# A state-space mixer whose TensorE order is written out by hand: eight products per run, dense slices between them, and a projection that ends half by half

## The chip, the core and the metric

The kernel runs on one core of a Trainium2 chip. It works with five engines, each with a queue of its own that it takes in order: TensorE (matmuls, PE in the profile, with its weight loads as PEld), VectorE (DVE), ScalarE (ACT), GpSimd (POOL) and SyncE (SP), which here issues nearly all transfers between device memory and the on-chip memory. The metric is the device time of one execution in microseconds; a kernel is told by the median of its runs.

## What is computed

One layer of a streaming encoder on a sequence of 1024 positions of width 1024, in float32. One input projection feeds two branches, whose outputs are gated, added and projected; a SwiGLU sub-layer follows.

```python
proj = h @ w_in
y_a = sparse_mla_attention(...) @ w_o_attn
y_b = ssd_mixer(z, xbc, dt_raw, ...) @ w_o_ssd
mix = (sigmoid(g_a) * y_a + sigmoid(g_b) * y_b) @ w_out
x = x + gate_m * rmsnorm(mix, post_norm_mix)
f = (silu(u_gate) * u_up) @ w_ffn_out
x = x + gate_f * rmsnorm(f, post_norm_ffn)
```

The change lies in the stretch that computes the state-space branch: for 8 groups of 4 heads the sequence is worked through in chunks. Within a chunk, with decay matrix `Lmat` and inputs `X`, and with the state `prev` that earlier chunks leave:

```python
CB = einsum('bclgn,bcsgn->bcgls', Cc, Bc)
y_diag = einsum('bcgls,bcgrls,bcsgrp->bclgrp', CB, Lmat, X)
states = einsum('bclgn,bcgrl,bclgrp->bcgrpn', Bc, decay, X)
y_off = einsum('bclgn,bcgrpn,bcgrl->bclgrp', Cc, prev, exp(a_cum))
y = y_diag + y_off + d_skip * xh
return rmsnorm(y * silu(z), ssd_norm)
```

The kernel uses chunks of 256 positions instead of 64, which gives the same sums.

## The kernel before

Activations lie with channels on the 128 partitions and positions along the free dimension, in two halves of 512 positions (`b` is 0 or 1). A dense product is made in float32 accuracy from three matmuls per 128 x 128 tile: each operand is split into a high part (a copy in the format fp32r) and a low part (the rest), and high x high, high x low and low x high are added. A half of one output tile over 1024 inputs is thus 24 matmuls of 128 x 128 by 128 x 512 (`dense`, or `dense_steps`, a generator that yields after every six). Splits are made by `split_to` (high on ScalarE at L246, low on VectorE or GpSimd at L247); weights come through `Stream` (transfer at L150, high on ScalarE at L151, low on GpSimd at L152), up to three split tiles at a time.

On-chip memory is handed out from arenas, each a number of equal slots: H with 32 slots of 512 columns, Q with 26 of the same size, R with 8 of 1024, EV with 9 of 512. A slot is used again when all readers of the tile in it are through.

After the attention come 32 steps, one for each pair of group and chunk, group outermost. A step has two parts, both generators:

- `ssd_in` loads B, C and x (`ld`, L961 and L962) and the cumulated decay, spread over all partitions (`al`, L967), takes relu and exp of the decay on ScalarE (L972, L973, L975), and makes on TensorE the product of B and C (`pcb`, L978 and L979), the transposed x (`px`, L989) and, but for the last chunk, the transposed B (`pbn`, L998). VectorE masks pcb (`cbm`, L981), multiplies it into the decay, which gives M in the tiles `al` and `M` (L983), and scales x (`X`, L991); GpSimd weighs X with the decay to the end of the chunk (`Xd`, L1002). It yields after each piece: four pieces.
- `ssd_out` loads z and the decay from the start of the chunk into one tile (`zy`, L1013 and L1016), multiplies M and X (`pyd`, L1022 and L1023, products of half the array's columns, four with 256 columns and four with 128), Xd and B (`pst`, L1029), and the state and C (`pyo`, L1034). VectorE adds these up (L1036, L1037, L1041), GpSimd multiplies by z (L1043), the result is stored (`d_y`, L1044), its squares are summed for the norm (L1047, L1053), and the state is brought forward (L1057, L1059). It has four pieces as well; the first ends in the middle of pyd.

`weave` calls the pieces of `ssd_in` for one step and of `ssd_out` for the step before in turn, and calls the generator `beside` between them, four times per step. `beside` is dense work that the mixer doesn't need: eight tiles of the input projection for one of the gates (`pw`, two halves each, input Hs, the split h, which fills all 32 slots of H), then the loads and splits of the attention's output (`atl`, L1078, into H), then eight tiles of the attention's output projection (`poa`, two halves each, evacuated at L1087). That is 32 products of four slices each, 128 slices.

This order of calls isn't the order on the engines. A planner, which simulates the program with costs of its own, takes the traced instructions and orders each engine's queue anew, as operands, slots and engines come free in its simulation. The context `in_order` chains the instructions of an engine in the order in which they were traced, and so takes this freedom away on that engine for the code inside; instructions from outside can still be put between. The mixer stands in an `if True:` without it.

After the mixer `y_load` loads y, half by half, scales and splits it (`yh` on ScalarE at L1125, `yw` on VectorE at L1126, into H, 32 slots for the 16 tiles of a half), and `merge` multiplies it by `w_o_ssd` (`pos`, 48 matmuls per tile, weights through the same `Stream`).

Of the kernel before, what the change touches and what calls it, by code (L numbers as in the profile page):

```python
# [11 lines left out]
F32R = mybir.dt.float32r  # L12
# [13 lines left out]
D_INNER, SSD_HEADS, GROUPS = 2048, 32, 8  # L26
# [12 lines left out]
NCH = L // QC  # L39
LAST = ((0, 0, 512), (1, 0, 256), (1, 256, 256))  # L40
FFN_GROUPS = [4, 4, 4, 4, 3, 3]
EARLY = 18

COLS = {}
_n = 0
# [22 lines left out]
def build(tc, a, dbg=None, stop=99, slots=None):  # L68
# [9 lines left out]
    H_ = Arena(ctx, tc, "H", n_slots["H"], 512)  # L78
# [7 lines left out]
    def bank_d(name):  # L86
        return pd.tile([P, 512], F32, name=name, tag="d", bufs=3)
# [7 lines left out]
    def half(b):  # L95
        return slice(512 * b, 512 * b + 512)
# [74 lines left out]
    def col_tile(w):  # L171

        kt = w.shape[1]
        return [(w[:, k:k + min(4, kt - k)], min(4, kt - k)) for k in range(0, kt, 4)]
# [55 lines left out]
    def dense_steps(o, b, w, xs, n=6):  # L230

        i = 0
        for (hi, lo), k0, ks in w:
            for j, k in enumerate(ks):
                for wt, xi in ((hi, 0), (hi, 1), (lo, 0)):
                    T.matmul(o, wt[:, k0 + j, :], xs[k][xi][b], start=i == 0, stop=i == 23)
                    i += 1
                    if i % n == 0 and i < 24:
                        yield

    def wpieces(ks, n=4):

        return [(W.next(), 0, ks[i:i + n]) for i in range(0, len(ks), n)]
# [5 lines left out]
    def split(alloc, src, name, shape=None, lo_eng=None):  # L249
        hi = alloc(name + "h", shape, F32R)  # L250
        lo = alloc(name + "l", shape, F32R)
        split_to(src, hi, lo, lo_eng)
        return hi, lo
# [569 lines left out]
    def weave(x, nx, y, ny, z=iter(()), nz=0, lead=1):  # L823

        i = j = k = 0
        while i < nx or j < ny:
            if j >= ny or (i < nx and i * ny <= j * nx * lead):
                next(x, None)
                i += 1
            else:  # L830
                next(y, None)
                j += 1
            while k < nz and k * (nx + ny) < nz * (i + j):
                next(z, None)
                k += 1
        for g in (x, y):
            for _ in g:
                pass
# [167 lines left out]
    def ssd_out(c, g, z):  # L1006
# [12 lines left out]
        for j in range(2):  # L1019
            for e in range(2):  # L1020
                o = pyd[64 * e:64 * e + 64, 256 * j:256 * j + 256]
                T.matmul(o, X[:, 0, 2 * j + e], M[j][:, e], start=True, stop=False, skip_group_check=True)  # L1022
                T.matmul(o[:, 128:256], X[:, 1, 2 * j + e], M[2][:, 2 * j + e], start=False, stop=True, skip_group_check=True)  # L1023
            if j == 0:
                yield
        if c < NCH - 1:
            pst = bank("pst")
            for t in range(2):
# [33 lines left out]
    def beside():  # L1062

        for t in range(8):
            W.plan(col_tile(a["w_in"][57 + t]))
            w = wpieces(ks8)
            for b in BS:
                p = bank_d("pw")
                yield from dense_steps(p, b, w, Hs)
                o = EV("g")  # L1070
                S.activation(o, p, AF.Copy)
                SP.dma_start(d_gb[t][:, half(b)], o)
                yield
        AT = [([None, None], [None, None]) for _ in range(KT)]
        for b in BS:
            for k in range(KT):
                t = EV("atl")
                SP.dma_start(t, d_att[k][:, half(b)])  # L1078
                AT[k][0][b], AT[k][1][b] = split(H_, t, "at", lo_eng=G if k % 2 else V)
        for t in range(8):  # L1080
            W.plan(col_tile(a["w_o_attn"][t]))
            w = wpieces(ks8)
            for b in BS:
                ya = EV("ya")
                p = bank_d("poa")
                yield from dense_steps(p, b, w, AT)
                V.tensor_copy(ya, p)  # L1087
                SP.dma_start(d_ya[t][:, half(b)], ya)
                yield

    filler = beside() if stop != 3 else iter(())
    if True:
        prev = None
        for s_ in [(c, g) for g in range(GROUPS) for c in range(NCH)] + [None]:
            z = {}
            weave(ssd_in(*s_, z) if s_ else iter(()), 4 if s_ else 0, ssd_out(*prev) if prev else iter(()), 4 if prev else 0, filler, 4)
            prev = s_ and (*s_, z)
        for _ in filler:
            pass
# [20 lines left out]
    def y_load(b, ks, places):  # L1120
        for k in ks:
            t = EV("yl")
            SP.dma_start(t, d_y[k][:, half(b)])
            yh, yw = places("yh", dt=F32R), places("yw", dt=F32R)
            S.activation(yh, t, AF.Copy, scale=col("ssd_norm", k))  # L1125
            V.scalar_tensor_tensor(yw, t, col("ssd_norm", k), f(yh), op0=OP.mult, op1=OP.subtract)  # L1126
            YB[b][k] = ([yh] * 2, [yw] * 2)
# [121 lines left out]
        t = R(name, (P, 2, 512), F32R)  # L1249
        return t[:, 0], t[:, 1]  # L1250

    y_load(0, range(16), H_)
    rys = []
    for b in BS:
        rys.append(wp.tile([P, 4, P], F32, name="rys", tag=("uraw", "uh")[b], bufs=1).rearrange("p k m -> p (k m)"))
        S.activation(rys[b], rbank(ysq[b], D_INNER), AF.Copy)
    MG = merge(0, in_r)
    y_load(1, range(16), H_)
    x1 = []
    for _ in residual_steps(0, *mixed(0, MG), x1):  # L1260
        pass
# [259 lines left out]
```

## Time and profile before

| | us |
|---|---|
| runs, median (lowest to highest) | 2464.05 (2463.94 to 2467.35) |
| span of the profiled execution | 2459.8 |
| median of the runs above that span | 4.25 |
| TensorE busy in the span | 2383.1 (97%) |
| VectorE, ScalarE, GpSimd busy | 1496.3, 1183.7, 1022.3 |
| first pcb of the mixer to its last | 1141.7 to 1486.1 |
| first and last poa | 1301.6 and 1458.1 |
| first pos | 1463.2 |

In the views of the profile L12 is line 12 of the kernel; a row names the tile that is written and those that are read. Matmuls overlap in the pipeline, so the distance from start to start tells what one costs, not its duration; a product in plain float32 shows as two records. In views by stretch of time a row has the busy time of each engine, the granted clock of TensorE (1.00 is full speed), the busy share of the 16 DMA engines and GB/s. A row of waits has the waiting instruction, what released it, the sum, how many, and the longest. Rows of transfers have the size in KB and the median time from issue to landing.

### The profile page before, as it was taken

What the parts mean: (1) busy time and instruction counts of PE and PEld (TensorE: products, weight loads), DVE (VectorE), ACT (ScalarE), POOL (GpSimd) and SP (SyncE); (2) the same over time, 40 slices, a digit from 0 to 9 for tenths busy, and PEclk for the clock granted to TensorE, in tenths of its full rate; (3) what the DMA queues carried; (4) which work ended last, traced back from release to release, by engine and by line L of the source; (5) the groups of instructions that cost most, each with busy time, mean ns of one, the idle gap of its engine ahead of it and who ended that gap; (6) DMA issues with size and microseconds to landing.
All of it is one profiled execution on the core that took longest, in us unless ns stands there. A gap on an engine that the chain in (4) does not pass through costs nothing. (4 is left out here: it accounts for less than half of the span.)

```text
span 2459.8 us, 34881 instructions
## 1 busy us (share of the span) xinstructions
PE 2383.1 (97%) x11946; PEld 1931.1 (79%) x11946; DVE 1496.3 (61%) x3050; ACT 1183.7 (48%) x2285; POOL 1022.3 (42%) x829
## 2 busy tenths in 40 slices
PE   7999999999999999999999999999999999999996
PEld 5788888888788887777776767888777888888886
DVE  4566775698745556765558666455476666552336
ACT  4446665567445545556566565544454222352211
POOL 2722112222234334553336335656676555432233
PEclk9999999999999999999999999999999999999998
DMA  7224122523212222223768775654465444253132
GB/s 268 99 77 130 65 73 78 155 87 103 86 67 92 102 99 91 93 84 123 223 215 260 228 246 172 231 186 161 168 208 171 160 145 163 99 190 113 48 99 90
DMA packets 212834, 341.25 MB, mean 139 GB/s; under 512 B 21249, under 2 KB 85425, under 8 KB 212657
## 3 DMA queue, kind: packets, MB, share of 16 engines
q1 hardware_dynamic: 211936, 338.45, 41.6%
q8 instruction: 94, 1.54, 0.3%
q14 instruction: 84, 0.68, 0.1%
q10 hardware_dynamic: 720, 0.58, 0.1%
HBM read 254.77 MB, written 87.32 MB: 139 GB/s over the span
## 5 line engine op out<-in xcount | busy, mean ns | idle before, releaser
L152 POOL TENSOR_TENSOR wlo<-wraw,whi 128x512 fp32r<-128x512 f32 (+1 forms) x282 | 380.7, 1351 | 769.4 <-ACT whi L151 698.5
L151 ACT ACTIVATE whi<-wraw 128x512 fp32r<-128x512 f32 (+1 forms) x282 | 175.4, 623 | 319.0 <-PE pfo L226 110.5
L1283 PE MATMUL p<-xh,wr 128*128 128x512 f32 x880 | 274.4, 391 | 3.8 <-DVE g L1333 3.6
L1283 PEld LDWEIGHTS p<-xh,wr 128*128 128x128 f32 x880 | 165.8, 188 | 39.1 <-DVE g L1333 4.0
L1277 POOL TENSOR_TENSOR wr<-a,wr 128x512 fp32r<-128x512 f32 x110 | 152.7, 1402 | 103.6 <-ACT wr L1276 70.6
L1283 PE MATMUL p<-xl,wr 128*128 128x512 f32 x440 | 171.8, 391 | 0.0
L778 ACT ACTIVATE lg<-lg,mx 128x256 f32<-128x256 f32 (+7 forms) x128 | 98.2, 769 | 74.7 <-DVE mx L775 73.5
L1276 ACT ACTIVATE wr<-a 128x512 fp32r<-128x512 f32 x110 | 67.7, 628 | 123.1 <-PE p L1283 98.0
L226 PE MATMUL pfo<-ah,wlo 128*128 128x512 f32 x304 | 118.1, 389 | 0.0
L226 PE MATMUL pfo<-al,whi 128*128 128x512 f32 x304 | 117.9, 389 | 0.0
L226 PE MATMUL pfo<-ah,whi 128*128 128x512 f32 x304 | 117.8, 389 | 0.0
L317 POOL TENSOR_TENSOR adaw<-adaw,cs 128x512 f32<-128x512 f32 x64 | 66.7, 1044 | 114.7 <-DMA adaw<-ada_w 109.4
L1398 DVE TENSOR_TENSOR facc<-facc,pfo 128x512 f32<-128x512 f32 x64 | 43.9, 686 | 112.0 <-PE pfo L226 112.0
L1283 PE MATMUL p<-h2h,wr 128*128 128x512 f32 x352 | 111.1, 393 | 0.0
L638 ACT ACTIVATE junk<-acc,cand__2203 128x1024 bf16<-128x1024 f32 (+2 forms) x96 | 86.2, 898 | 45.5 <-DVE cand__2203 L681 28.0
L226 PE MATMUL pos<-yw,whi 128*128 128x512 f32 x256 | 101.7, 397 | 3.6 <-DVE yw L1126 3.6
L226 PE MATMUL pos<-yh,whi 128*128 128x512 f32 x256 | 101.4, 396 | 1.7 <-ACT yh L1125 1.7
L226 PE MATMUL pos<-yh,wlo 128*128 128x512 f32 x256 | 101.5, 397 | 1.1 <-POOL wlo L152 1.1
L589 DVE SCALAR_TENSOR_TENSOR acc<-rel,widx,acc 128x384 f32<-128x384 f32 (+2 forms) x90 | 87.0, 986 | 24.9 <-ACT rel L584 24.7
L584 ACT ACTIVATE rel<-prel 128x512 f32<-128x512 f32 (+3 forms) x160 | 77.3, 524 | 48.4 <-PE prel L583 44.8
L1283 PEld LDWEIGHTS p<-xl,wr 128*128 128x128 f32 x440 | 83.0, 189 | 17.4
L799 PE MATMUL pt<-ident,lg 128*128 128x128 f32 x576 | 87.4, 277 | 7.1 <-ACT lg L778 6.6
(573 smaller groups left out, 6978.2 us busy)
## 6 DMA issues: line engine op xcount, KB each, us to landing
wraw<-w_in SPq DMA_DIRECT2D x130, 256.0 KB, 2.6
a<-w_ffn_in SPq DMA_DIRECT2D x124, 256.0 KB, 3.0
adaw<-ada_w SPq DMA_DIRECT2D x64, 256.0 KB, 2.7
al<-d_ac SPq DMA_DIRECT2D x32, 512.0 KB, 5.8
wraw<-w_o_ssd SPq DMA_DIRECT2D x64, 256.0 KB, 3.2
al<-d_a SPq DMA_DIRECT2D x44, 256.0 KB, 5.3
d_a<-g SPq DMA_DIRECT2D x40, 256.0 KB, 2.5
ada<-ada_p SPq DMA_DIRECT2D x16, 512.0 KB, 6.5
```

Of the source, the lines that this page charges most:

```text
L151: behind(S.activation(hi[:, :kt], raw[:, :kt], AF.Copy))
L152: behind(G.tensor_tensor(lo[:, :kt], raw[:, :kt], f(hi[:, :kt]), op=OP.subtract))
L226: T.matmul(o, wt[:, k0 + i, :], xs[k][xi][b][:, sl], start=pi == 0 and i == 0 and wt is hi and xi == 0, stop=pi == len(pcs) - 1 and i == l ...
L317: behind(G.tensor_tensor(t, t, cs[:, 4 * h:4 * h + 4, None].to_broadcast([P, 4, P]), op=OP.mult))
L584: S.activation(rel[:, 512 * b:512 * b + w_], pr[:, 0:w_], AF.Relu)
L589: V.scalar_tensor_tensor(acc[i][:, 0:n], rel[:, 0:n], ws, acc[i][:, 0:n], op0=OP.mult, op1=OP.add)
L638: S.activation(jk, y, AF.Sign, scale=-1.0, bias=a_, accum_out=o)
L778: S.activation(lg[:, 0:n], lg[:, 0:n], AF.Exp, scale=-1.0, bias=m, accum_out=mx[:, 3:4])
L799: T.transpose(ptv[:, hh, t, :], PR[hh, t][:, j * P:(j + 1) * P], ident)
L1276: S.activation(w[:, 0], src, AF.Copy)
L1277: G.tensor_tensor(w[:, 1], src, f(w[:, 0]), op=OP.subtract)
L1283: T.matmul(p, w[:, wi, i], X[x][i][xi], start=start and i == 0 and k == 0, stop=i == 3 and k == 2, skip_group_check=True)
```

## The change

Three things are done together. The mixer's TensorE instructions are put into `in_order`, so they go in the traced order. For that order the yield inside pyd is taken out, so all eight products of a step follow each other, `ssd_out` counts as three pieces, and the dense work is called four and three times in turn instead of four. Whatever of it is left after the last step follows there, inside the same order. The attention's projection takes tiles 0 to 4 with both halves each, and then tiles 5 to 7 with the first half and once more with the second, for which their weights are loaded again. The split input of the projection goes to Q for the first four tiles of the first half, and the split y of tiles 8 to 11 of the first half goes to Q as well.

```diff
+POA_BOTH = 5
+AT_IN_Q = 4
+Y_IN_Q = range(8, 12)
...
                 T.matmul(o[:, 128:256], X[:, 1, 2 * j + e], M[2][:, 2 * j + e], start=False, stop=True, skip_group_check=True)
-            if j == 0:
-                yield
...
-                AT[k][0][b], AT[k][1][b] = split(H_, t, "at", lo_eng=G if k % 2 else V)
-        for t in range(8):
-            W.plan(col_tile(a["w_o_attn"][t]))
-            w = wpieces(ks8)
-            for b in BS:
-                ya = EV("ya")
...
+                AT[k][0][b], AT[k][1][b] = split(Q if b == 0 and k < AT_IN_Q else H_, t, "at", lo_eng=G if k % 2 else V)
+        for ts, bs in [((t,), BS) for t in range(POA_BOTH)] + [(range(POA_BOTH, 8), (b,)) for b in BS]:
+            for t in ts:
+                W.plan(col_tile(a["w_o_attn"][t]))
+                w = wpieces(ks8)
+                for b in bs:
+                    ya = EV("ya")
...
-    if True:
+    with in_order(mybir.EngineType.PE):
         prev = None
-        for s_ in [(c, g) for g in range(GROUPS) for c in range(NCH)] + [None]:
+        for n, s_ in enumerate([(c, g) for g in range(GROUPS) for c in range(NCH)] + [None]):
             z = {}
-            weave(ssd_in(*s_, z) if s_ else iter(()), 4 if s_ else 0, ssd_out(*prev) if prev else iter(()), 4 if prev else 0, filler, 4)
+            weave(ssd_in(*s_, z) if s_ else iter(()), 4 if s_ else 0, ssd_out(*prev) if prev else iter(()), 3 if prev else 0,
+                  filler, 4 - n % 2)
...
-            yh, yw = places("yh", dt=F32R), places("yw", dt=F32R)
+            where = places(k)
+            yh, yw = where("yh", dt=F32R), where("yw", dt=F32R)
...
-    y_load(0, range(16), H_)
+    y_load(0, range(16), lambda k: Q if k in Y_IN_Q else H_)
...
-    y_load(1, range(16), H_)
+    y_load(1, range(16), lambda k: H_)
```

More of the change, by code (lines that the diff above doesn't have):

```diff
@@ L1078, in beside @@
                 SP.dma_start(t, d_att[k][:, half(b)])
-                AT[k][0][b], AT[k][1][b] = split(H_, t, "at", lo_eng=G if k % 2 else V)
-        for t in range(8):
-            W.plan(col_tile(a["w_o_attn"][t]))
-            w = wpieces(ks8)
-            for b in BS:
-                ya = EV("ya")
[L1085 to L1089, printed above, removed]
+                AT[k][0][b], AT[k][1][b] = split(Q if b == 0 and k < AT_IN_Q else H_, t, "at", lo_eng=G if k % 2 else V)
[5 more added lines that the diff above has]
+                    ya = EV("ya")
+                    p = bank_d("poa")
+                    yield from dense_steps(p, b, w, AT)
+                    V.tensor_copy(ya, p)
+                    SP.dma_start(d_ya[t][:, half(b)], ya)
+                    yield
     filler = beside() if stop != 3 else iter(())
-    if True:
+    with in_order(mybir.EngineType.PE):
         prev = None
-        for s_ in [(c, g) for g in range(GROUPS) for c in range(NCH)] + [None]:
+        for n, s_ in enumerate([(c, g) for g in range(GROUPS) for c in range(NCH)] + [None]):
             z = {}
-            weave(ssd_in(*s_, z) if s_ else iter(()), 4 if s_ else 0, ssd_out(*prev) if prev else iter(()), 4 if prev else 0, filler, 4)
+            weave(ssd_in(*s_, z) if s_ else iter(()), 4 if s_ else 0, ssd_out(*prev) if prev else iter(()), 3 if prev else 0,
+                  filler, 4 - n % 2)
             prev = s_ and (*s_, z)
```

## The prediction

> **What bounds the kernel now.** I read the page first, then the busy time by stretch around the state-space mixer, then the waits of TensorE in the two stretches that stood out, then the order of time on TensorE within one step.
>
> ```profile
> span 2459.8 us, 34881 instructions
> ```
>
> ```profile
> core 0: us, PE busy (x) PEld busy (x) DVE busy (x) ACT busy (x) POOL busy (x), PEclk, DMA share, GB/s
> 1290.00:1320.00 30.00, 24.81 (x118) 17.58 (x117) 24.02 (x29) 20.14 (x42) 19.37 (x14) 0.89 0.98 310
> 1460.00:1480.00 20.00, 14.71 (x65) 9.14 (x64) 15.40 (x23) 17.03 (x35) 4.75 (x4) 0.74 1.00 325
> 1180.00:1290.00 110.00, 110.00 (x598) 85.81 (x598) 63.64 (x101) 67.21 (x149) 40.93 (x34) 1.00 0.68 218
> 1340.00:1450.00 110.00, 110.00 (x599) 85.88 (x598) 74.17 (x117) 59.12 (x132) 43.90 (x36) 1.00 0.72 230
> ```
>
> In the two long stretches TensorE has no idle time at all and the full clock: there only fewer or cheaper TensorE instructions can gain, and no other engine is near its limit. The two short stretches are seams. At 1290 to 1320 it idles 30.00 - 24.81 = 5.2 us, and the granted clock of 0.89 costs about 0.11 x 24.81 = 2.7 us more: 7.9 us. At 1460 to 1480 it idles 5.3 us and loses 0.26 x 14.71 = 3.8 us to the clock: 9.1 us. Both have the DMA engines at a share of 0.98 and 1.00. The waits name the seams:
>
> ```profile
> PE poa L236 <- ACT ath L246: 3.2, 2, 3.0
> PE poa L236 <- POOL atl L247: 1.2, 1, 1.2
> ```
>
> ```profile
> PE pos L226 <- DVE yw L1126: 3.6, 3, 2.3
> PE pos L226 <- ACT yh L1125: 1.7, 1, 1.7
> ```
>
> The first is the attention's projection waiting for its split input, which can be written only once the split h (Hs) has left arena H. The second is the merge's first product waiting for the split of y, which takes H after the projection is through with it.
>
> At 1460 the Trainium skill ("TensorE: Matmul & The Clock Gate", Why this matters for your kernels) would say otherwise: it lets the clock fall after idle gaps of more than about 3 us between bursts. The longest wait here is 2.3 us, and the clock fell to 0.74 all the same, so the row decides; by the rule the second seam would be worth only its 5.3 us of idle time, and the sum below would be 12.2 us in place of 16 (2451.8). Since the row contradicts it, that case gets no chance of its own.
>
> **The order within a step.** These are consecutive rows of TensorE in one step, dense slices at both ends.
>
> ```profile
> 1186.88 0.39 PE L236 MATMUL pw<-h5h,wlo 128*128 128x512 f32 x1
> 1187.11 0.39 PE L236 MATMUL pw<-h6h,whi 128*128 128x512 f32 x1
> 1187.42 0.66 PE L1022 MATMUL pyd<-al,X 128*64 128x256 f32 x4
> 1187.91 0.40 PE L1023 MATMUL pyd<-M,X 128*64 128x128 f32 x4
> 1188.23 0.70 PE L978 MATMUL pcb<-ld 128*128 128x256 f32 x2
> 1188.77 0.38 PE L979 MATMUL pcb<-ld 128*128 128x128 f32 x2
> 1189.08 0.66 PE L1022 MATMUL pyd<-al,X 128*64 128x256 f32 x4
> 1189.56 0.40 PE L1023 MATMUL pyd<-M,X 128*64 128x128 f32 x4
> 1189.89 0.66 PE L989 MATMUL px<-ident,ld 128*128 128x128 f32 x4
> 1190.38 1.03 PE L1034 MATMUL pyo<-ld,state 128*128 128x256 f32 x4
> 1191.25 0.38 PE L998 MATMUL pbn<-ident,ld 128*128 128x128 f32 x2
> 1191.38 0.48 PE L236 MATMUL pw<-h6l,whi 128*128 128x512 f32 x1
> 1191.70 0.40 PE L236 MATMUL pw<-h6h,wlo 128*128 128x512 f32 x1
> ```
>
> The planner cuts the half-width products (128*64) into two runs with other work between. A dense matmul takes 0.23 us from start to start; 256 columns of a full-width product take 0.87 / 4 = 0.22 us (pyo), 128 columns 0.49 / 4 = 0.12 (px). Into a half-width run it takes 0.31 instead of 0.23, so 0.08 more; inside, the L1022 part takes 0.49 where two steps of 0.22 are due, 0.05 more; out of it 0.32 where two of 0.12 are due, 0.08 more. A run of its own thus costs about 0.2 us. Going from full-width state-space work to dense costs nothing that shows: from 1191.25 to 1191.70 are 0.45 us, which two steps of 0.11 and one of 0.23 fill.
>
> **The change, part by part.** *Eight products per run* removes one run in each of 32 steps: 32 x 0.2 = 6.4 us (4.8 to 7.7 for 0.15 to 0.24 each), on the path because TensorE has no idle time there. *Fixed order, slices between* adds no instruction. It puts the slices of six, four and three in turn, between the pieces, so the dense work no longer runs ahead: 116 of its 128 slices are used up by the 33 turns, and 12, three products of 24 matmuls or 3 x 24 x 0.23 = 16.5 us, come after the last state-space product. They are not extra work; they lie where the second seam is. *Half by half* for t = 5, 6, 7 lets the first half's split input go before these three products start; its slots in H, the eight slots of H that the projection no longer uses now that four k lie in Q, and Q for k = 8 to 11 then take the split y of twelve k ahead of time.
>
> ```profile
> L1125 ACT ACTIVATE yh<-yl,vec x32: 705/722/752, 1462.4 to 1602.4; 128x512 fp32r<-128x512 f32 x32
> L1126 DVE SCALAR_TENSOR_TENSOR yw<-yl,vec,yh x32: 735/748/1871, 1463.1 to 1605.8; 128x512 fp32r<-128x512 f32 x32
> ```
>
> Four of the twelve can go earlier still. The eight k that wait for the first half take 8 x 0.75 = 6 us on VectorE and less on ScalarE, inside the 16.5 us; the last four take 3 us while the merge's first product works on the twelve before them (36 x 0.23 = 8.3 us). So the second seam goes whole: 9.1 us, at least 5 if loads of y come late, since the DMA engines are full there.
>
> The three tiles of weights are loaded twice: six more loads of 256 KB with these splits,
>
> ```profile
> L152 POOL TENSOR_TENSOR wlo<-wraw,whi 128x512 fp32r<-128x512 f32 (+1 forms) x282 | 380.7, 1351 | 769.4 <-ACT whi L151 698.5
> L151 ACT ACTIVATE whi<-wraw 128x512 fp32r<-128x512 f32 (+1 forms) x282 | 175.4, 623 | 319.0 <-PE pfo L226 110.5
> ```
>
> 6 x 1.35 = 8.1 us on GpSimd and 6 x 0.62 = 3.7 on ScalarE. Both have a third or more of the time free in the long stretches, and behind a lo part at 1.35 us stand 12 matmuls, 2.8 us: nothing on the path. Were that cover gone, the six lo parts would cost up to 8 us.
>
> *Split input in both arenas.* Four of the first half's eight k can be split into Q before Hs is gone, and since the slices now come one product per step, the other slots of Hs come free a step before they are needed. What stays is the 16 x 0.26 = 4.2 MB of loads. The mixer's own traffic rises as its steps get shorter:
>
> ```profile
> L989 PE MATMUL px<-ident,ld x128: 272/273/328, 1144.3 to 1488.7; 128*128 128x128 f32 x128
> ```
>
> That is 31 steps in 344.4 us, 11.1 us each. A new step is 3.5 slices of 6 x 0.23 = 4.8 us and state-space products of about 4.1 (from 1187.42 to 1191.47 above, less 0.2, with pst in three of four steps): 8.9 us. The DMA share of 0.70 becomes 0.70 x 11.1 / 8.9 = 0.87, and near the seam four steps ask for 4 x 8.9 us x 280 GB/s + 4.2 MB, about 14 MB, or 43 us at the 325 GB/s of the fullest stretch, against 36 us; what is loaded ahead covers a part. I take 4.5 of the 7.9 us as won (0 to 7.9).
>
> **What the fixed order can cost.** The planner no longer fills a late operand with dense work. Two chains have to fit a step of 8.9 us. The first goes from pcb through VectorE and ScalarE to the next pyd:
>
> ```profile
> 1243.74 0.38 PE L979 MATMUL pcb<-ld 128*128 128x128 f32 x2
> ...
> 1253.65 0.66 PE L1022 MATMUL pyd<-al,X 128*64 128x256 f32 x4
> ...
> 1257.52 1.03 PE L1034 MATMUL pyo<-ld,state 128*128 128x256 f32 x4
> ```
>
> ```profile
> 1244.16 0.56 DVE L981 TENSOR_TENSOR cbm<-pcb,mask 128x384 f32<-128x384 f32 x1 [0.83 <-PE pcb L979]
> ...
> 1248.66 1.21 DVE L983 TENSOR_TENSOR al<-al,cbm 128x1024 f32<-128x1024 f32 x1
> ```
>
> ```profile
> 1246.08 1.04 ACT L975 ACTIVATE al<-al 128x1024 f32<-128x1024 f32 x1
> ```
>
> M is done 5.8 us after pcb (1249.87 - 1244.12) and pyd follows 3.8 us later. In the new order pyo, px, pbn and three slices lie between: 0.9 + 0.5 + 0.2 + 4.1 = 5.7 us. That just holds; 3 of the 5.8 us are the exponent, which can go earlier, so the chain could be 2.6 us. The second chain is the reload of zy:
>
> ```profile
> 1241.78 0.37 SPq L1044 DMA_DIRECT2D d_y<-zy  x1
> 1247.32 0.37 SPq L1013 DMA_DIRECT2D zy<-d_z  x1
> 1247.74 1.24 SPq L1016 DMA_DIRECT2D zy<-d_ea  x2
> ```
>
> ```profile
> d_y<-zy SPq DMA_DIRECT2D x32, 256.0 KB, 5.3
> zy<-d_ea SPq DMA_DIRECT2D x48, 128.0 KB, 3.3
> ```
>
> The next z is issued the moment that the store has landed, with everything behind it on SP's queue held for these 5 us, so slots are what limits the loads. The second ea lands at about 1252 and is used after pyo, at 1258.5: some 6 us of slack over two steps. Two steps shrink by 4.4 us, which leaves 1.5 to 2, less whatever fuller DMA engines add. So both chains fit with little room. I charge 4 us of new waits, 0.12 us a step; the ends are 0 and 22 (below).
>
> **The sum** against the profiled span: -9.1 (second seam) - 4.5 (first) - 6.4 (runs) + 4 (new waits) = -16.0 us, 2443.8. The runs' median stands 2464.05 - 2459.8 = 4.25 us above the span, so **2448 us**.
>
> **Rivals.** *Half of it*: the first seam stays, since the DMA engines are full, and of the second 5 us go: -5 - 6.4 + 4 = -7.4, 2456.7. For it: shares of 0.98 and 1.00 in both seams. Against it: part of the loads now comes ahead.
>
> *The reload of zy sets the step.* If landings lengthen by 1.5 us each at a share of 0.87 (5.3 to 6.8, 3.3 to 4.8), the loop of two steps is 22.2 - 6 + 3.0 = 19.2 us, 9.6 a step: 0.7 x 32 = 22 us given back, -20 + 22 = +2, 2466. For it: SP stands still 5 us a step as it is. Against it: 218 GB/s and 230 GB/s gave the same TensorE, with no wait.
>
> *Slower*: pyd waits for M in every step, because the planner leaves the exponent after pcb as now. From a chain of 5.7 + 20 / 32 = 6.3 us upward it eats all the gain of 20 us; at 6.7 us it costs 32 x 1.0 = 32, +12, 2476. For it: 5.8 us today, and ScalarE is the engine that also evacuates the dense products. Against it: SP issues the loads as soon as slots come free (its rows above), so al is there ahead of pcb and the exponent can move forward.
>
> **Numbers.** Forecast 0.42, more than that (no new waits, both seams whole, -23) 0.05, half of it 0.18, zy's loop 0.16, slower 0.19. A measurement of this kernel tells about 0.2%, 5 us, from no change. Faster: the first two and nine tenths of the third, 0.63; same: zy's loop and the rest of the third, 0.18; slower 0.19. The range goes from 2438 (all won and a little from the planner's new order elsewhere) to 2471, which leaves out the worse two thirds of the slower case; the forecast's own is 2441 to 2455.
>
> **What would show it.** In the changed profile: L1022 in runs of eight records with no pcb between; no wait of pos for yh or yw over 1 us, and the last poa after the last pyo; the granted clock at 1.00 where the merge starts; the first wait of poa on ath shorter than 3.0 us; px from first to last over some 280 to 290 us instead of 344. Waits of pyd on L983, of pcb on ld, or idle TensorE of more than 5 us inside the mixer would be the new waits. The forecast is wrong if the mixer's steps stay above 9.9 us, for then nothing is won.

## The result, and the profile after

The changed kernel takes **2493.2 us** (median of 4 runs, 2492.2 to 2494.3) against 2463.99 us before: a ratio of 1.0118, 95% interval 1.0103 to 1.0132. The forecast was 2448, with a range up to 2471. The page of the changed kernel begins with its span; before it was 2459.8 us.

```profile
span 2492.5 us, 34910 instructions
```

Busy time of the changed kernel in four stretches from the mixer to the merge (columns as in the prediction: busy time and instructions of each engine, granted clock, share of the DMA engines, GB/s):

```profile
1180.00:1290.00 110.00, 100.39 (x569) 80.10 (x569) 75.17 (x106) 69.94 (x158) 46.03 (x34) 0.98 0.69 218
1290.00:1320.00 30.00, 26.22 (x153) 20.91 (x153) 22.38 (x32) 16.10 (x37) 11.59 (x9) 1.00 0.68 197
1320.00:1450.00 130.00, 109.42 (x580) 85.75 (x580) 87.69 (x125) 72.48 (x159) 58.12 (x43) 0.93 0.71 227
...
1480.00:1520.00 40.00, 35.95 (x171) 29.55 (x172) 15.91 (x28) 14.24 (x27) 17.47 (x15) 0.93 0.43 140
```

Before, TensorE was busy all through 1180 to 1290 and 1340 to 1450 and idle only in the two seams. Now every stretch shown has idle time. The share of the DMA engines hardly moved (0.69 and 0.71 in the first and third row, against 0.68 and 0.72 in the long stretches before). The same view over the whole of the mixer and both seams, first before and then after:

```profile
1130.00:1530.00 400.00, 387.44 (x2077) 295.57 (x2076) 261.99 (x401) 238.45 (x513) 167.00 (x131) 0.98 0.69 218
```

```profile
1130.00:1530.00 400.00, 355.69 (x1949) 280.30 (x1948) 256.92 (x394) 229.36 (x499) 163.42 (x123) 0.97 0.67 212
```

Idle time grew by 387.4 - 355.7 = 31.7 us, nearly the whole loss of 32.7 us in the spans. The clock adds about 0.03 x 355.7 - 0.02 x 387.4 = 3 us, rounded as these clocks are. Over the whole span TensorE is busy for 2382.9 us against 2383.1 before, so its idle time (2492.5 - 2382.9 against 2459.8 - 2383.1) grew by 32.9 us: the loss is idle time. The steps of the mixer, which were to shrink to 8.9 us, take (1486.4 - 1150.6) / 31 = 10.8 us:

```profile
L992 PE MATMUL px<-ident,ld x128: 270/272/273, 1150.6 to 1486.4; 128*128 128x128 f32 x128
```

The waits of TensorE between 1130 and 1560 in the changed kernel say where (time, how often, longest):

```profile
PE pst L1030 <- POOL Xd L1005: 21.8, 11, 5.0
PE pyd L1025 <- DVE al L986: 10.2, 7, 2.2
PE poa L239 <- ACT ath L249: 4.5, 1, 4.5
PE pyd L1025 <- DVE X L994: 2.7, 3, 1.7
PE pos L229 <- ACT yh L1129: 2.4, 1, 2.4
PE pos L229 <- DVE yw L1130: 0.7, 1, 0.7
```

The largest, pst (the state's product) waiting for Xd, was in no term of the forecast. The waits of pyd for M (al), which it did reckon with, come second. The waits of both seams (poa, pos) are still there.

What stands behind it, in one step of the changed kernel (start, duration, engine, line; rows of four engines, in order of time, others left out at the dots):

```profile
1209.99 0.60 PE L992 MATMUL px<-ident,ld 128*128 128x128 f32 x4
...
1211.70 0.68 DVE L994 TENSOR_TENSOR X<-px,dt 128x512 f32<-128x512 f32 x1
...
1213.01 0.88 DVE L1042 SCALAR_TENSOR_TENSOR zy<-ld,dsk,zy 128x256 f32<-128x256 f32 x2
...
1214.02 1.27 POOL L1044 TENSOR_TENSOR zy<-zy 128x512 f32<-128x512 f32 x1 [2.00 <-DVE zy L1042]
...
1214.65 0.44 PE L1026 MATMUL pyd<-M,X 128*64 128x128 f32 x4
1215.25 1.04 POOL L1005 TENSOR_TENSOR Xd<-X,decay 128x512 f32<-128x512 f32 x1
1215.32 0.63 ACT L1048 ACTIVATE ysqt<-zy 128x512 f32<-128x512 f32 x1 [4.25 <-POOL zy L1044]
1215.86 0.36 ACT L1003 ACTIVATE bn<-pbn 128x256 f32<-128x256 f32 x1
...
1216.37 1.11 PE L1030 MATMUL pst<-Xd,bn 128*128 128x256 f32 x4 [1.28 <-POOL Xd L1005]
```

X is ready at 1212.38, but on GpSimd Xd stands behind the product of y with z of the step before (L1044), for which the engine stood idle 2.00 us until VectorE had done zy at L1042. Xd ends at 1216.29 and pst starts at once. On ScalarE the other operand, bn, stands behind ysqt, which waits for the same product. The Trainium skill ("Perfetto Trace Analysis", Tensor Engine Instruction) calls the execution queues of ScalarE, VectorE and GpSimd strict FIFO; this row agrees, for X was ready 2.9 us before Xd started.

The trace shows the same in all eleven waits of pst for Xd: between X and Xd GpSimd runs the product with z. In three of them nothing else stands there. In seven a low weight part (wlo, L155, about 1.3 to 2.3 us) comes in as well, and in the longest, of 5.0 us, two splits of the attention's output (atl). So it is the whole queue ahead of Xd that makes it late, with the product with z in every case.

Before, the corresponding rows were these (kernel before, same view):

```profile
1233.88 0.65 PE L989 MATMUL px<-ident,ld 128*128 128x128 f32 x4
...
1235.34 1.42 POOL L1002 TENSOR_TENSOR Xd<-X,decay 128x512 f32<-128x512 f32 x1 [1.57 <-DVE X L991]
...
1240.46 1.29 POOL L1043 TENSOR_TENSOR zy<-zy 128x512 f32<-128x512 f32 x1
...
1244.86 1.13 PE L1029 MATMUL pst<-Xd,bn 128*128 128x256 f32 x4
```

There Xd stood ahead of the product with z, and pst came 11.0 us after px, 8 us after Xd was done. The change took out the yield between the two runs of pyd. That joined the runs, but it also pulled pst, which is written behind them, from the second piece of a step into the first: it is now asked for before the next step's px, and in the median it starts 6.4 us after its own px instead of 10.3 (table below).

### The profile page after: what moved, and what is told of

It reads as the page before. It is cut to its first block, busy times and chain, and to the rows that moved or that the text cites. A ratio compares the mean times of both kernels' runs of the same rounds, so it can differ in the third digit from the quotient of the medians.

```text
span 2492.5 us, 34910 instructions
## 1 busy us (share of the span) xinstructions
PE 2382.9 (96%) x11946; PEld 1942.2 (78%) x11946; DVE 1500.9 (60%) x3050; ACT 1188.7 (48%) x2291; POOL 1036.9 (42%) x835
## 5 line engine op out<-in xcount | busy, mean ns | idle before, releaser
L155 POOL TENSOR_TENSOR wlo<-wraw,whi 128x512 fp32r<-128x512 f32 (+1 forms) x288 | 390.7, 1357 | 739.7 <-ACT whi L154 675.4
```

The costliest lines, as they stand in the source:

```text
L155: behind(G.tensor_tensor(lo[:, :kt], raw[:, :kt], f(hi[:, :kt]), op=OP.subtract))
```

## The experiments

All times are medians of four to twelve runs, with the ratio to the kernel before on the same chip and its 95% interval. The px row of each kernel (first to last of the transposes, 31 steps) gives the length of a step.

**First batch: which part of the change costs the time.** a_order_only keeps the fixed order, the runs of eight and the turns, and drops the halves and the arenas. b_halves_only does the opposite. c_run8_only is the kernel before with the yield taken out. d_pst_late is the changed kernel with pst put behind px, in the third piece.

```diff
--- changed kernel
+++ a_order_only
-POA_BOTH = 5
-AT_IN_Q = 4
-Y_IN_Q = range(8, 12)
+POA_BOTH = 8
+AT_IN_Q = 0
+Y_IN_Q = range(0)
```

> The fixed TensorE order, the runs of eight and the slices four and three in turn, but the projection with both halves of each tile together, its weights loaded once, and every split input in H, as before the change. Queue theory (the fixed order meets the order that the planner gave GpSimd, VectorE and ScalarE: Xd stands behind the product with z on GpSimd, M behind other work, and TensorE has nothing else to do): the waits of pst and pyd inside the mixer stay, some 40 us of them, the second seam is open again, 2490 to 2503 us. Load theory (fuller DMA engines and the reload of zy make operands late): the same total, but with waits that trace back to transfers. Halves theory (the second loading of weights, SP's queue and the arenas cost the time): 2455 to 2466 us.

```diff
--- changed kernel
+++ b_halves_only
+            if j == 0:
+                yield
...
-    with in_order(mybir.EngineType.PE):
+    if True:
...
-            weave(ssd_in(*s_, z) if s_ else iter(()), 4 if s_ else 0, ssd_out(*prev) if prev else iter(()), 3 if prev else 0,
-                  filler, 4 - n % 2)
+            weave(ssd_in(*s_, z) if s_ else iter(()), 4 if s_ else 0, ssd_out(*prev) if prev else iter(()), 4 if prev else 0,
+                  filler, 4)
```

> The projection half by half with its weights loaded twice for three tiles, and the split inputs in both arenas, but no fixed order, the yield inside pyd and four slices a step as before the change. Queue and load theories: no waits of pst or pyd on TensorE, 2458 to 2470 us, as the planner again fills with dense work; the seams may move by a few us either way. Halves theory: most of the 29 us, 2480 us or more.

```diff
--- kernel before
+++ c_run8_only
-            if j == 0:
-                yield
...
-            weave(ssd_in(*s_, z) if s_ else iter(()), 4 if s_ else 0, ssd_out(*prev) if prev else iter(()), 4 if prev else 0, filler, 4)
+            weave(ssd_in(*s_, z) if s_ else iter(()), 4 if s_ else 0, ssd_out(*prev) if prev else iter(()), 3 if prev else 0, filler, 4)
```

> Only the yield inside pyd is taken out (and three pieces counted); the planner orders TensorE freely, everything else as before the change. If a half-width run of its own costs 0.2 us, 32 fewer give -6.4 us, 2458 us, all theories alike; 2462 or more would say that the runs are not worth what the records of one step gave, or that the planner cuts them again.

```diff
--- changed kernel, ssd_out
+++ d_pst_late
-        if c < NCH - 1:
-            pst = bank("pst")
-            for t in range(2):
-                T.matmul(pst[:, 0:256], z["bn"][:, t], z["Xd"][:, t].rearrange("p h n -> p (h n)"), start=t == 0, stop=t == 1)
         yield
...
         yield
+        if c < NCH - 1:
+            pst = bank("pst")
+            for t in range(2):
+                T.matmul(pst[:, 0:256], z["bn"][:, t], z["Xd"][:, t].rearrange("p h n -> p (h n)"), start=t == 0, stop=t == 1)
         sq = Q("ysqt", (P, 2, 256))
```

> The changed kernel with pst moved in the fixed order from right behind pyd to behind px, some 4 us later in the step. Queue theory: the 22 us of waits of pst for Xd go, and no more than a third of them come back as waits of pyd or pyo; 2468 to 2478 us. Load theory: Xd isn't what is late, so other waits take their place, 2488 us or more.

Measured: a 2496.4 us, 1.0122 [1.0101, 1.0143]; b 2480.7, 1.0061 [1.0040, 1.0081]; c 2505.7, 1.0162 [1.0143, 1.0181]; d 2475.9, 1.0045 [1.0029, 1.0062].

So a has the whole loss, with the same waits (pst for Xd 16.9 us, pyd for M 10.3): the halves and arenas are not needed for it and do not mend it. By themselves (b) they lose 15 us, which lies at the edge of what the halves theory said (2480 or more), so they are not free where the planner orders TensorE. No wait of pst is among b's; its waits lie elsewhere: pyd for M 6.9 us, poa for ath 6.0, pos 5.4 for a weight's high part and 4.3 for y. Why they come was not tried. And d wins back 17 of the 29 us. Its largest waits of TensorE in the same stretch:

```profile
PE pyd L1025 <- DVE al L986: 15.4, 13, 2.2
PE poa L239 <- ACT ath L249: 7.2, 1, 7.2
PE pyd L1025 <- DVE X L994: 3.2, 1, 3.2
```

No wait of pst is left, and that for M has grown from 10.2 to 15.4 us: the second chain comes forward where the first is mended. c was the worst miss, since it was to win the 6 us of the runs. Its rows of the attention's projection and of px, then the last stretch of its mixer:

```profile
L236 PE MATMUL poa<-ath,whi x128: 387/389/502, 1291.6 to 1427.6; 128*128 128x512 f32 x128
```

```profile
L989 PE MATMUL px<-ident,ld x128: 272/273/273, 1152.1 to 1545.1; 128*128 128x128 f32 x128
```

```profile
1500.00:1560.00 60.00, 34.69 (x192) 26.33 (x190) 36.49 (x59) 29.41 (x62) 19.27 (x17) 0.84 0.46 149
```

With seven pieces in a turn and no order held, the planner used the dense work up by 1428, and the mixer ran on until 1545, at the end nearly without cover: 25 of 60 us idle and a clock of 0.84. Waits of pst for Xd are there as well (5.9 us, none before), although no order is held. What the missing piece does to the planner was not tried further.

**Second batch: the late operand, and the loads.** f puts Xd on VectorE. g joins the first two pieces of ssd_in, so that pcb comes ahead of the pyd of the step before. h adds to g loads that are written earlier (four attention inputs two tiles, that is four products, ahead; twelve loads of y ahead of the last three products). In the cut of h, `at_load` is the loop of these loads made a function, and `y_load` is moved up unchanged. i is the changed kernel without the loads of ea: it leaves out the factor that they bring.

```diff
--- changed kernel
+++ f_xd_on_dve
-            G.tensor_tensor(Xd, X, decay[:, 2 * c:2 * c + 2, hs, None].to_broadcast([P, 2, 4, 64]), op=OP.mult)
+            V.tensor_tensor(Xd, X, decay[:, 2 * c:2 * c + 2, hs, None].to_broadcast([P, 2, 4, 64]), op=OP.mult)
```

> The changed kernel with Xd made by VectorE (about 0.7 us) instead of GpSimd; TensorE's order is untouched. Queue theory: Xd no longer stands behind the product with z and the low weight parts, so the 22 us of waits of pst go; VectorE gets 0.7 us a step more, so the waits of pyd may grow by some us: 2470 to 2482 us. Load theory: X or other operands are late, and the waits stay: 2488 us or more.

```diff
--- changed kernel, ssd_in and the loop
+++ g_pcb_first
             S.activation(m, m, AF.Exp, scale=-1.0)
-        yield
         pcb = bank("pcb")
...
-            weave(ssd_in(*s_, z) if s_ else iter(()), 4 if s_ else 0, ssd_out(*prev) if prev else iter(()), 3 if prev else 0,
+            weave(ssd_in(*s_, z) if s_ else iter(()), 3 if s_ else 0, ssd_out(*prev) if prev else iter(()), 3 if prev else 0,
```

> The changed kernel with the first two pieces of ssd_in made one, so that in the fixed order pcb of a step goes ahead of pyd of the step before, and px and pbn move up with it: the way from pcb to the next pyd and from px to the next pst gets some 3 us longer, while the work stays the same. Queue theory: both kinds of waits inside the mixer go, what stays are the seams: 2448 to 2462 us. Load theory: pcb needs its loads 3 us earlier, so waits of pcb for ld appear, 2485 us or more.

```diff
--- g_pcb_first
+++ h_early_loads
         for t in range(8):
+            if t == 6:
+                at_load(0, range(AT_IN_Q))
             W.plan(col_tile(a["w_in"][57 + t]))
...
+        y_load(0, range(12), lambda k: Q if k in Y_IN_Q else H_)
         for _ in filler:
             pass
...
-    y_load(0, range(16), lambda k: Q if k in Y_IN_Q else H_)
+    y_load(0, range(12, 16), lambda k: H_)
```

> As the kernel with pcb first, and the loads at both seams are traced earlier: the first four tiles of the attention's output two tiles of the gate projection ahead, and twelve tiles of y ahead of the three last products. If the seams stay open because the planner puts these loads behind others on SP's queue, the waits of poa on ath and of pos on yh shrink by 5 to 12 us against the kernel with pcb first: 2438 to 2452 us. If the DMA engines are what is full there, nothing changes by more than 3 us.

```diff
--- changed kernel, ssd_out
+++ i_no_ea
-        if c:
-            for e in range(2):
-                SP.dma_start(yt[64 * e:64 * e + 64],
-                             d_ea[c, hs].rearrange("(j e) l -> e j l", e=2)[e:e + 1].to_broadcast([64, 2, QC]))
...
-            V.tensor_tensor(ytf, ytf, pyo, op=OP.mult)
+            V.tensor_tensor(ytf, zc.rearrange("p j l -> p (j l)"), pyo, op=OP.mult)
```

> The changed kernel without the 48 loads of the decay from the start of the chunk: the product of state and C is multiplied by z's tile instead, which leaves that part of the computation out. The reload of zy then has one load of 3.3 us less and the DMA engines 14% less of the mixer's traffic. Load theory: most of the 29 us come back, 2465 to 2475 us. Queue theory: the waits of pst and pyd stay as they are, 2486 to 2495 us.

Measured: f 2495.6 us, 1.0119 [1.0090, 1.0148]; g 2467.6, 1.0015 [1.0003, 1.0026]; h 2466.3, 1.0010 [1.0001, 1.0020]; i 2492.7, 1.0121 [1.0100, 1.0142].

i speaks against the loads: with 48 loads of 128 KB gone the share of the DMA engines between 1180 and 1450 falls from 0.70 to 0.63, but TensorE's idle time there is the same (34.0 and 34.5 us) and the waits stay (pst for Xd 16.8 us, pyd for M 10.3). f missed, and its waits say why:

```profile
PE pst L1030 <- ACT bn L1003: 13.5, 8, 3.2
PE pyd L1025 <- DVE al L986: 12.3, 7, 2.5
```

The wait went over to bn, pst's other operand, which stands directly behind ysqt on ScalarE in all eight, as in the rows of the changed kernel. g has no wait of pst, 11.6 us for M and steps of (1458.7 - 1150.9) / 31 = 9.9 us; it came out 6 us above its expectation. h closed the second seam, but its 1.3 us less than g are within the intervals: new waits came near the first seam, pbn for cbm 4.1 us, pyd for M up to 5.2 us.

**Third batch: the order by itself, M, and the mends together.** j is the kernel before with TensorE's order fixed as it is written, nothing else. m is the changed kernel with the runs of eight undone. k is g with VectorE's order fixed too. l takes g, pst of d and the loads of y of h together.

```diff
--- kernel before
+++ j_fixed_only
-    if True:
+    with in_order(mybir.EngineType.PE):
--- changed kernel
+++ m_runs_of_four
+            if j == 0:
+                yield
...
-            weave(ssd_in(*s_, z) if s_ else iter(()), 4 if s_ else 0, ssd_out(*prev) if prev else iter(()), 3 if prev else 0,
+            weave(ssd_in(*s_, z) if s_ else iter(()), 4 if s_ else 0, ssd_out(*prev) if prev else iter(()), 4 if prev else 0,
--- g_pcb_first
+++ k_vec_order
-    with in_order(mybir.EngineType.PE):
+    with in_order(mybir.EngineType.PE, mybir.EngineType.DVE):
```

> The kernel before with its own pieces and turns (runs of four, four pieces, four slices a turn), only with TensorE's order fixed as it is written down. Theory (the loss comes from pst and pyd being asked for one piece too early, not from an order being fixed): pst stands behind the second pcb piece as before, its waits on Xd and bn stay below 3 us in all, those of pyd on M below 8 us; 2458 to 2474 us. Rival (a fixed order as such costs the stalls, because TensorE can no longer fill with dense work): at least 2485 us, pyd and pst waiting 20 us or more in all.

> The changed kernel with only the runs of eight undone: the half-width products are cut into two runs of four again and the state's products (pst) come behind the second, in four pieces. Theory (merging pulled pst one piece forward, in front of Xd and bn): the waits of pst go (below 3 us in all), 32 x 0.2 = 6 us of extra runs come back; 2470 to 2482 us, faster than the change by 10 to 20 us. Rival (the loss sits elsewhere in the order): at least 2490 us.

> pcb ahead of the previous step's pyd as in g_pcb_first, and VectorE's order inside the mixer fixed as written too, so that cbm and the products with the exponents (M) stand ahead of the previous step's zy, dsk and state work. Theory (pyd waits for M because the planner puts M behind that work on VectorE): the waits of pyd on M fall from 11.6 us to below 4, the steps of px from 9.9 us to 9.3 to 9.6, 2450 to 2462 us. Rival (VectorE, held in an order, waits itself for late operands, and what stands behind is late): 2470 us or more, with TensorE's waits moved to cbm, X or ya.

> Three mends at once: pcb ahead of the previous step's pyd, pst a piece later, and twelve loads of y written ahead of the three last attention products; the loads of the first seam stay as in the change. Theory: the second seam's waits of pos go (about 3 us against g_pcb_first) and pst never waits; pyd's waits on M stay at about 12 us; 2460 to 2467 us, no measurable gain on the kernel before. Rival (the seams or M give way further): below 2456 us.

Measured: j 2475.2 us, 1.0043 [1.0031, 1.0055]; m 2496.1, 1.0129 [1.0116, 1.0142]; k 2543.0, 1.0320 [1.0305, 1.0334]; **l 2453.9, 0.9958 [0.9946, 0.9971]**.

j: a fixed order costs 11 us even with the pieces of before, with waits for M of 13.6 us; pst does not wait there. The time is just above what the theory gave (2474), the waits for M are well above its 8 us. So about 11 of the 29 us are of the order as such. a costs some 20 more; what it has beside j is the merged run with pst drawn forward, and three slices in every second turn.

m was the surprise. It has no wait of pst, as expected, and is no faster, so its rival came true. Its largest wait:

```profile
PE pyd L1025 <- DVE al L986: 25.5, 14, 4.1
```

m also stands 21 us above j, although its runs are apart like j's. What it has beside j are the three slices in every second turn and the halves with their arenas. So the 20 us between j and a cannot be put down to merging alone: fewer slices between the pieces could do it too, and no run has the merged runs with four slices in a fixed order. How the 20 us divide stays open.

That a mend brings another wait is understandable, as the planner plans the other three engines anew around every order of TensorE. The following table is worked out from the starts and ends of these instructions in the traces, the first pcb with the first pyd of its step and so on: medians over the 32 steps, in the last two rows over the 24 steps that have Xd and pst, in us; distances are from the start of pcb or px.

```
                       before  after  runs of four (m)  no gate (o)  best (l)
pcb to first relu       -1.0   -3.0        +1.3            -2.8        +3.5
pcb to M done            6.3    4.9         8.0             3.9        10.5
pcb to its pyd          10.6    6.4         9.8             6.3        12.0
px to Xd done            3.2    5.3         2.9             4.1         3.2
px to its pst           10.3    6.4         9.6             5.3        12.9
```

The distances to pyd and pst include the waits. In l both are long because pcb and px of a step go ahead of pyd and pst of the step before. In m the relu ahead of the exponent starts 1.3 us after pcb in place of 3.0 before it, so M is late: what the forecast called the slower case, and argued against because the exponent can go forward, happened here.

k fell, by far: fixing VectorE's order makes TensorE wait for X (36.1 us) and for the state (20.9 us).

```profile
1204.39 0.42 DVE L1053 TENSOR_TENSOR ysq<-ysq,ysqt 128x256 f32<-128x256 f32 x1 [3.80 <-ACT ysq L1051]
1204.74 0.55 DVE L983 TENSOR_TENSOR cbm<-pcb,mask 128x384 f32<-128x384 f32 x1
...
1207.94 1.22 DVE L985 TENSOR_TENSOR al<-al,cbm 128x1024 f32<-128x1024 f32 x1 [2.65 <-ACT al L978]
```

VectorE itself stood idle for 3.80 and 2.65 us for ScalarE, with X behind (it started at 1210.76). So it is not shown that an order on VectorE would bring M earlier, and what puts M late in the mended kernels stays open.

l is the version that beats both kernels, by 10 us and by 39. The expectation had it level with the kernel before; the rival came true. Its largest waits of TensorE in the stretch:

```profile
PE pyd L1024 <- DVE al L985: 8.2, 7, 2.2
PE poa L239 <- ACT ath L249: 7.5, 1, 7.5
```

Neither pst nor pos waits any more, and px goes from 1151.1 to 1450.5 us, 9.66 a step.

**Fourth batch: what was left open.** o takes the product with z out of the changed kernel, and so leaves out the gate. p is l with runs of four. q is l with the early attention inputs of h.

```diff
--- changed kernel, ssd_out
+++ o_no_gate
-        G.tensor_tensor(yt, yt, zc, op=OP.mult)
--- l_g_pst_y
+++ p_l_fours
+            if j == 0:
+                yield
...
-            weave(ssd_in(*s_, z) if s_ else iter(()), 3 if s_ else 0, ssd_out(*prev) if prev else iter(()), 3 if prev else 0,
+            weave(ssd_in(*s_, z) if s_ else iter(()), 3 if s_ else 0, ssd_out(*prev) if prev else iter(()), 4 if prev else 0,
--- l_g_pst_y, beside
+++ q_l_at_early
+            if t == 6:
+                at_load(0, range(AT_IN_Q))
```

> The changed kernel without the product with z on GpSimd; it leaves out the gate of y by z, and so its output differs. Theory (Xd on GpSimd and, through ysqt, bn on ScalarE stand behind that product): the waits of pst fall from 21.8 us to below 5, although pst keeps its place; the waits of pyd on M may grow, so 2468 to 2485 us. Rival (pst is late because X itself is late, whatever stands ahead of Xd): the waits of pst stay above 12 us, at least 2487 us.

> The fastest version so far (l_g_pst_y, 2453.9 us) with its runs of eight cut into two runs of four again, nothing else. It prices the run by itself, away from the stalls. The forecast's price: 32 x 0.2 = 6.4 us, so 2458 to 2463 us. Rival (the second run shifts the chains, as in m_runs_of_four, and M is waited for): 2466 us or more, with the waits of pyd on M above 15 us. Rival (a run costs nothing where TensorE waits anyway): below 2457 us.

> l_g_pst_y with the loads and the split of the four attention inputs that lie in Q written two products ahead, as in h_early_loads. Theory (8.5 us of waits at the first seam are of SP's order, not of the DMA engines): those waits fall below 3 us; 2444 to 2450 us. Rival (as in h_early_loads, VectorE is crowded by the splits and cbm or M comes late instead): 2451 to 2456 us, with new waits of pbn, X or M at 1285 to 1350.

Measured: o 2466.6 us, 1.0003 [0.9991, 1.0016]; p 2477.9, 1.0042 [1.0028, 1.0055]; q 2454.2, 0.9942 [0.9929, 0.9955].

o shows what makes pst late. Its waits fall from 21.8 to 8.1 us in all (its four rows: 4.0, 2.2, 1.5, 0.4), with pst in its place. The theory had them below 5; where Xd still comes late in o, it stands behind low weight parts or splits. The time falls by 26.6 us, more than was expected, and only 13.7 us of this are pst's waits: those of pyd for M fell too, from 10.2 to 1.7 us, where the expectation had them grow, if anything. Why M comes sooner was not traced. The same step as above, now in o:

```profile
1211.61 0.68 DVE L994 TENSOR_TENSOR X<-px,dt 128x512 f32<-128x512 f32 x1
...
1212.36 1.05 POOL L1005 TENSOR_TENSOR Xd<-X,decay 128x512 f32<-128x512 f32 x1 [0.44 <-DVE X L994]
...
1214.66 0.36 ACT L1003 ACTIVATE bn<-pbn 128x256 f32<-128x256 f32 x1
1215.16 1.10 PE L1030 MATMUL pst<-Xd,bn 128*128 128x256 f32 x4 [0.18 <-ACT bn L1003]
```

X comes at the same time within 0.1 us, and Xd starts 0.07 us behind it, where in the changed kernel it starts 2.87 us behind it. In this step it is not X that is late but the place behind the product with z.

p prices the runs. Busy time over the mixer and both seams, l and then p:

```profile
1130.00:1530.00 400.00, 382.03 (x2120) 305.29 (x2120) 254.50 (x411) 244.95 (x527) 190.15 (x141) 0.99 0.72 228
```

```profile
1130.00:1530.00 400.00, 373.38 (x2033) 287.92 (x2032) 250.80 (x406) 238.68 (x514) 164.69 (x133) 0.97 0.68 218
```

The spans are 2453.1 and 2475.1 us, 22.0 apart. Idle time takes 382.0 - 373.4 = 8.7 of it (the wait for M went from 8.2 to 21.2 us, that for ath fell) and the clock about 0.03 x 373.4 - 0.01 x 382.0 = 7.4, which leaves 5.9 us for 32 runs, 0.18 each; the rounding of the clocks makes that uncertain by up to 4 us. The time of 2458 to 2463 was missed and the first rival came true: the second run moved M again, as in m.

q's waits for the split input at the first seam fell from 8.5 to 3.3 us, so the order in which the loads are written does set that wait. But the time is that of l, as the rival had it (2451 to 2456). In its profiled execution first to last px take 296.8 us against 299.4 in l, while q enters the mixer 5.9 us later (first px at 1157.0 against 1151.1). These 5.9 us have nothing to do with the seam: 5.0 of them are there 140 us into the span, where both kernels run the same instructions. By the ratios, each to the kernel before on its own chip, q is 0.16% ahead of l, 4 us, with intervals that overlap. So what the seam is worth stays open, between nothing and some 4 us.

## Why the prediction was wrong

**What bounds the kernel** was read rightly: TensorE without idle time, and so only fewer TensorE instructions or the seams to be won. What was not drawn from it is the other side: the late operands of the mixer were hidden by the planner's freedom to slip dense work in, and the change takes it away. Taking only that away costs 11 us (j).

**Runs of eight, -6.4 us.** As a price this held. In the changed kernel a run of eight (each product leaves two records) goes from 1203.26 to 1204.73, where pst begins:

```profile
1203.26 0.66 PE L1025 MATMUL pyd<-al,X 128*64 128x256 f32 x4 [0.17 <-ACT M L975]
1203.71 0.43 PE L1026 MATMUL pyd<-M,X 128*64 128x128 f32 x4
1203.93 0.65 PE L1025 MATMUL pyd<-al,X 128*64 128x256 f32 x4
1204.36 0.44 PE L1026 MATMUL pyd<-M,X 128*64 128x128 f32 x4
1204.73 1.13 PE L1030 MATMUL pst<-Xd,bn 128*128 128x256 f32 x4
```

That is 1.47 us; the two runs of before, from 1187.42 to 1188.23 and 1189.08 to 1189.89, are 1.62, and one entry of 0.08 lies ahead of the run besides: 0.23 us won. p gave 0.18 where stalls were mended. But what stands behind the second run came with it: the forecast counted pst among the products of a step and never asked that it is moved a piece forward.

**Fixed order, +4 us of new waits (0 to 22).** This is the step that failed. Measured: 21.8 us of pst and 10.2 + 2.7 = 12.9 of pyd, 34.7 in all, beyond the upper end. The forecast named two chains that have to fit, pcb to M to pyd and the reload of zy. The first was sized well in the median: counted from the end of pcb as in the forecast, M is done after 4.2 us (5.8 before, with the exponent moved ahead of pcb as it said) and pyd comes after 5.6 (5.7 in the forecast). But the steps differ: from the start of pcb M takes 3.3 to 8.6 us, and the slow ones cost the 10 us. The second does not bind: none of TensorE's waits is put down to it, and without its loads of ea nothing changes (i). A third, px to X to Xd or bn to pst, was left out, though its slack could be read from the trace of before: 8 us between the end of Xd and pst, of which 0.1 us are left in the median. The forecast looked only at the distance on TensorE and at each operand's own duration; it never asked what stands ahead of Xd on GpSimd. That pst's waits come from there is shown (o, and d, which moves pst away from them); what makes M late in the slow steps, and how the loss beyond j's 11 us divides between the merged run and the fewer slices, is not.

A smaller slip: the forecast's step of 8.9 us counts 4.1 us of state-space products. By its own rows, 4.05 - 0.2 us with pst (0.97 us, 1244.86 to 1245.83) in three of four steps and pyo and pbn taken out of one in four, they come to about 4.3. The step enters only the DMA share and the room of the chains, not the sum.

**Second seam, -9.1 us.** Mostly not won. Between 1480 and 1520 TensorE idles 4.1 us and loses 0.07 x 36.0 = 2.5 us to the clock, 6.6 in place of 9.1. As forecast the last poa (1513.89) comes after the mixer, and three products lie where the seam was. But the loads of y are issued too late for them to cover. On SP's queue in the changed kernel:

```profile
1510.48 3.05 SPq L153 DMA_DIRECT2D wraw<-w_o_ssd  x2
1513.58 0.90 SPq L1126 DMA_DIRECT2D yl<-d_y  x2
```

They stand behind loads of weights that wait for their slots: between 1490 and 1520 these waited 21.3 us on SP for low parts (wlo) on GpSimd. The forecast took only "if loads of y come late" at 5 us, for full DMA engines; the share there is 0.43. Written ahead of the three products (l), the first loads go at 1463.0 and the seam is gone, with a full clock:

```profile
1480.00:1520.00 40.00, 40.00 (x186) 33.25 (x185) 13.70 (x19) 17.45 (x28) 25.14 (x20) 1.00 0.60 192
```

So the three products do cover the seam, and the place of the loads in the queue was missed.

**First seam, -4.5 us.** Nothing won: 4.5 us of waits for ath and 0.5 for atl, against 4.9 before. The split into Q did not come ahead, since all sixteen loads are issued from 1327.08 on. Full DMA engines were the reason given for half the price, and the share was not full (0.83 between 1320 and 1360); with the loads written earlier (q) the waits fell to 3.3 us.

**The rivals.** The fuller DMA engines are out: shares stayed at 0.68 to 0.71 in the first three stretches. Nothing points at the reload of zy: without its loads of ea nothing changes; its load of z was not taken out. The slower case had the right sign and a part of the cause (10 us of M), the wrong main chain, and stopped at 2476.

**The sum again.** 31.7 us of idle time, 3 of clock, less 6.4 for the runs are 28 of the 32.7 us between the spans; some 4 us stay unplaced, 1.2 of them idle time outside this stretch. For l the same sum is +5.4 idle, -4 clock, -6.4 runs: -5.0 of -6.7 us.

## What to carry to other kernels

A yield or a merge that is meant for one group of products moves everything written behind it: list for each product that moves what its operands wait for on their own engines, and what stands in those queues ahead of them. Under a planner, the late operands of a loop are covered by free work that slips in; before an order is fixed, every operand's slack has to be read from the trace (end of the operand to start of its user) and compared with the new distance, and one mended chain only brings up the next. A load that is to be covered by the last work of a stage has to be written ahead of that work's own loads on the same queue.

## What was not expected of the hardware

The granted clock fell at waits of about the same length in one place and not in another. In the changed kernel TensorE idles 2.2 to 3.6 us in each of these stretches of 10 us:

```profile
1290.00:1300.00 10.00, 7.61 (x47) 5.90 (x46) 7.27 (x11) 3.39 (x9) 4.91 (x4) 1.00 0.63 197
1350.00:1360.00 10.00, 6.42 (x25) 5.36 (x26) 5.65 (x8) 5.12 (x12) 4.12 (x4) 0.83 0.67 210
1410.00:1420.00 10.00, 7.78 (x39) 5.94 (x38) 7.55 (x10) 8.30 (x18) 6.22 (x4) 0.83 0.62 197
```

The second follows a wait of 5.0 us for Xd; in the third 2.2 us of idle time go with a clock of 0.83, in the first 2.4 us with a full one. The wait of the first goes on to 1300.27, 2.7 us in all, and the 10 us behind it have a full clock too. What decides it was not tried.
